# Within-chunk mLSTM products and token sums by 64 columns, gate products of all chunks in one, and 1/rms along tokens by DMA

## The chip, the cores and the metric

The kernel runs on one core of one Trainium2 chip. The metric is the device time of one execution, in microseconds (us). TensorE (PE) multiplies, VectorE (DVE) and ScalarE (ACT) do elementwise work, GpSimd (POOL) does small powers and memsets and issues part of the DMAs, SyncE (SP) issues the weight loads. A matmul keeps one operand in the array (stationary, loaded by a weight load, PEld) and streams the other through it. An f32 matmul appears in the trace as two passes, each with its own weight load; a transpose, and a matmul on the rounded fp32r type, is one pass.

## The reference

Two layers on x of 512 tokens by 1024. Each layer adds a mixer with four branches to x and then a squared-relu MLP; both read an RMSNorm of x. The parts that the change touches:

```python
def rms_norm(x, g):
    return x * lax.rsqrt(mean(x * x, -1) + EPS) * g

# mLSTM, chunks of 128 tokens, 4 heads of 64; i = c_i + i_bias, f = c_f + f_bias
b = cumsum(log_sigmoid(f))                       # within the chunk
dmat = where(tril, b_j - b_s + i_s, -inf)
mj = max(b + m_st, max_s dmat)
a = exp(dmat - mj) * (q @ k.T)
num = w_inter * (q @ c_st) + a @ v               # a @ v: the within-chunk product
den = w_inter * (q @ n_st) + sum(a)
h = num / max(abs(den), exp(-mj))
```

## The kernel before

The activations live feature-major, as 8 tiles of 128 features by 512 tokens. Every projection is a product of fp32 operands that are split in a high and a low fp32r part and multiplied in three passes (`mm3`: high·high, high·low, low·high). The weights stream from DRAM in chunks of mostly 512 KB: SP loads `raw` (two buffers), ACT casts it to `whi`, DVE subtracts to get `wlo` (three buffers each, `split_w`, lines 254 to 261). A layer is a fixed sequence of such products on PE: token-major groups (`tk`, 512, 336 or 256 columns), feature-major groups (`fm`), the gates (`g`, `p`), the output projection (`wo`), and the MLP (`up`, `q`, `r`).

All smaller work (indexer, attention, mLSTM, spatial gating, norms) is written as generators in a list `side`. After every half of a feature-major group, and twice per token-major weight chunk, `tick()` (lines 281 to 286) advances each generator to its next `yield`. What a generator issues is tied by `Paced` to the last projection pass before that tick, so it can't stand earlier than that on its engine. Within that, the order of each engine's queue is laid out when the program is built, by priority (`HP`, `Ahead`) and by when operands are due. At run time each queue is in order: an instruction that waits holds all behind it on its engine.

The places that the change touches:

- **Token sums.** `rstd2` (line 316) and `rstd` (line 332) get the mean square of each token: the sum of squares `acc` (128 by 512, over features) is multiplied by a column of 1/1024. The four blocks of 128 tokens of `acc` are the stationary operand, the moving one is a single column, and the result is `pa`, 128 tokens by 4. This is done four times: before each mixer and each MLP.
- **1/rms along tokens.** `rstd` raises the sums to the power -1/2 on POOL (`rs`, tokens on partitions), which the token-major projections use as a scale. For the feature-major ones it also needs 1/rms along the free axis on all partitions (`rb`, 128 by 512): lines 348 to 352 broadcast each column of `rs` as a stationary operand against the identity (`pb`, four f32 products) and ACT copies it to `rb`. The first reader is the `cqT` product of line 1171.
- **Gates.** `forget_gates` (line 905) computes the biased input gates `ip` and log-sigmoid forget gates `lf` for 128 tokens by 4 chunks by 4 heads, on DVE. `mlstm` (line 929) then takes the cumulative sum over a chunk twice: once with tokens on partitions (line 945, `bc`, one f32 product with the triangle `tri` as stationary), and once with heads on partitions (lines 958 to 960: for each chunk a product `br` with `lf` of that chunk, 4 columns, as stationary, and a transpose `ir` of `ip`). For each chunk DVE copies `br`, subtracts, and scans for the running maximum `Gr` (lines 961 to 967). `Gr` and the chunk maxima go through DRAM to be broadcast to all partitions (`MB`, `X`).
- **The within-chunk product.** In each chunk, lines 1033 to 1035 multiply the 128 by 128 matrix `X` of a head (stationary) by that head's 65 columns of values and ones (`vaug`), into `intra`. It follows the state product `inter` (64 rows of the array, from the second chunk on) and is followed, in the first three chunks, by the state update `U` (lines 1043 to 1045), whose 64 stationary columns go to one half of the output partitions or the other by head, as `half(h)` (line 662) says. The spatial gating's `mix` products (line 1233) are also of 64 columns.

POOL's queue holds, around the gates: the power `rs`, the tables `tab`, the power `va` of the indexer, the moves `qiA` and `qiB`, the power `ssq` of the query norm (line 1108), and the moves `qS`.

Of the kernel before, what the change touches and what calls it, by code (L numbers as in the profile page):

```python
# [13 lines left out]
F32 = mybir.dt.float32  # L14
# [7 lines left out]
P = 128  # L22
# [144 lines left out]
def trunk(tc, x_in, wall, consts, lps, sgus, out):  # L167
# [5 lines left out]
    with ExitStack() as es:  # L173
# [24 lines left out]
        xm_dram = [nc.dram_tensor(f"xm_{l}_dram", (KD, P, T), F32, kind="Internal").ap() for l in range(NL)]  # L198
        sum_dram = [nc.dram_tensor(f"sum_{l}_dram", (NC, P, D), F32, kind="Internal").ap() for l in range(NL)]
        gr_dram = [nc.dram_tensor(f"gr_{l}_dram", (4, T + 8), F32, kind="Internal").ap() for l in range(NL)]  # L200
        xs = [None]
# [69 lines left out]
        def pmm(o, a, b, start=True, stop=True):  # L271
            T_.matmul(o, a, b, start=start, stop=stop)
# [25 lines left out]
        def norm(x, gain, hh, hl, ks=range(KD), acc=None, sq_hp=True, sq_tile=None):  # L298
# [15 lines left out]
            return acc  # L314

        def rstd2(acc):

            r2 = small["t4"]

            def gen():  # L320
                yield
                yield
                pa = mmtile("pa", "ms")
                for c in range(NC):
                    pmm(pa[:, c:c + 1], acc[:, c * P:(c + 1) * P], ones)
# [6 lines left out]
        def rstd(acc, late=2):  # L332

            rs, t4 = small["rs"], small["t4"]
            rb = hpool.tile([P, T], F32, name="rb", tag="rb")

            def gen():
                for _ in range(late):
                    yield
                pa = mmtile("pa", "ms")  # L340
                for c in range(NC):
                    pmm(pa[:, c:c + 1], acc[:, c * P:(c + 1) * P], ones)
                with HP():
                    V.tensor_scalar(t4, pa[:, 0:4], EPS, None, ALU.add)
                    rpow(rs, t4)
                for _ in range(1 if late < 3 else 3):
                    yield
                pb = mmtile("pb", "ms")
                for c in range(NC):
                    pmm(pb[:, c * P:(c + 1) * P], rs[:, c:c + 1].to_broadcast([P, P]), ident)  # L350
                with HP():
                    S.copy(rb, pb)

            side.append(gen())
            return rs, rb
# [258 lines left out]
        for l in range(NL):  # L614
            with ExitStack() as em:
                x = mixer(tc, em, locals())
            hh, hl = htiles()
            r2 = rstd2(norm(x, lp("ln_mlp"), hh, hl))
            xs[0].close()
            if l < NL - 1:  # L620
                lpt = cpool.tile([P, NLP], F32, name="lp", tag="lp")
                nc.scalar.dma_start(lpt, lps[l + 1])
            nxt, acc = mlp(l, hh, hl, r2, lp("ln_mix"))
            if nxt:
                hh, hl = nxt
                rs, rb = rstd(acc, 8)
        flush()


def mixer(tc, em, env):  # L630
# [103 lines left out]
    else:  # L734
# [14 lines left out]
        load_consts()  # L749
        rs, rb = rstd(acc[0])  # L750
    qr = {}
# [153 lines left out]
    def forget_gates():  # L905
        s16 = [P, 4, 4]
        ip, lf, gc = (tt(s16, "c_" + n) for n in ("ip", "lf", "gc"))
        e5 = et("c_e")
# [16 lines left out]
        V.scalar_tensor_tensor(lf, pl, -2.0, fp, ALU.mult, ALU.add)  # L925
        lfs.extend((ip, lf, gc))
        yield

    def mlstm(yc):
# [11 lines left out]

        ip, lf, gc = lfs
# [12 lines left out]
        yield  # L955
        pr = mmtile("br", "ms")
        pi_ = mmtile("ir", "ms")
        for c in range(4):
            pmm(pr[0:4, blk(c)], lf[:, c], tri)
            ptr(pi_[0:4, blk(c)], ip[:, c])  # L960
        for c in range(4):
            br, gr = tt([4, P], "br"), tt([4, P], "gr")
            V.tensor_copy(br, pr[0:4, blk(c)])
            V.tensor_sub(gr, pi_[0:4, blk(c)], br)
            V.tensor_tensor_scan(Gr[:, blk(c)], gr, gr, ms8[:, c:c + 1], ALU.max, ALU.max)
            if c < 3:
                V.tensor_add(ms8[:, c + 1:c + 2], br[:, P - 1:P], Gr[:, c * P + P - 1:c * P + P])
        V.tensor_copy(ms8[:, 4:8], Gr[:, P - 1::P])

        G.dma_start(scr[:, 0:T], Gr)  # L970
        G.dma_start(scr[:, T:T + 8], ms8)
# [17 lines left out]
        for c in range(4):  # L989
            ptr(pe_[:, c * 4:c * 4 + 4], Gr[:, blk(c)])  # L990
        gcol = pe_[:, 0:16].rearrange("p (c h) -> p c h", h=4)
# [13 lines left out]
        for c in range(4):  # L1005
# [401 lines left out]
```

## Time and profile before

| | |
|---|---|
| median of 3 runs | 1596.76 us (1596.72 to 1596.97) |
| the profiled execution's own time | 1596.6 us |
| its span in the trace | 1594.8 us |
| PE busy | 1586.3 us, 99% of the span, 7510 passes |
| PEld, DVE, ACT, POOL busy | 82%, 70%, 45%, 8% |
| granted TensorE clock | 1.0 mean, 9 or more tenths in each of 40 slices |
| HBM traffic | 120 GB/s over the span |

The table's shares are means over the span. Passes on PE are pipelined: the time that a group of passes costs is read from start to start, not from the length of one pass. An idle time counts only where it is PE's.

### The profile page before, as it was taken

The numbers are of one execution on the slowest core, as the hardware profiler recorded it, in microseconds if no ns is written. First come the engines' busy times: TensorE is split into PE (matmuls) and PEld (weight loads), VectorE is DVE, ScalarE is ACT, GpSimd is POOL, SyncE is SP. The second block draws the span as 40 slices with busy tenths as digits, with TensorE's granted clock in tenths as the row PEclk, the third lists the DMA queues.
The fourth block names the chain that finished last, engine by engine and source line by source line (L and its number), as shares of the span: only waits on it lengthen the run. The fifth ranks groups of instructions, "written<-read, shape, count | busy, mean of one in ns | idle before, by whom it ended". The sixth has DMA issues, their size and how long they took to land.

```text
span 1594.8 us, 20013 instructions
## 1 busy us (share of the span) xinstructions
PE 1586.3 (99%) x7510; PEld 1310.9 (82%) x7510; DVE 1112.0 (70%) x1900; ACT 710.3 (45%) x1059; POOL 121.6 (8%) x141
## 2 busy tenths in 40 slices
PE   9999999999999999999999999999999999999998
PEld 8888888888888888888788888887888888888887
DVE  6899997545555655665988999975555557556568
ACT  5553234423345545635545432254233455456362
POOL 1212100000000100110013121000000001001100
PEclk9999999999999999999999999999999999999999
DMA  6433322242353473386443332322323524733844
GB/s 213 118 88 111 100 90 83 83 144 92 104 200 110 78 226 105 66 190 193 119 141 113 93 112 91 98 84 86 132 96 113 202 95 78 227 104 66 221 149 106
DMA packets 66129, 196.23 MB, mean 123 GB/s; under 512 B 7368, under 2 KB 14568, under 8 KB 66032
## 3 DMA queue, kind: packets, MB, share of 16 engines
q1 hardware_dynamic: 54160, 167.15, 31.7%
q0 software_dynamic: 11008, 26.79, 9.9%
q8 instruction: 59, 0.97, 0.2%
q10 hardware_dynamic: 864, 1.01, 0.2%
q14 instruction: 38, 0.31, 0.1%
HBM read 174.46 MB, written 16.79 MB: 120 GB/s over the span
## 4 chain that ended last, share of the span: by engine, by line
PE 88%; issue 9%; DMA 1%; POOL 1%; DVE 0%; ACT 0%; POOLq 0%; ACTq 0%; DVEq 0%
PE g L139 22%; PE up L139 16%; PE tk L139 11%; PE fm L139 8%; PE q L139 8%; PE p L139 6%; PE r L139 5%; PE wo L139 5%; DMA cr<-in_wall_dram 1%; PE ix L139 1%; POOL sum_dram L453 1%; PE lg L139 1%; PE av L139 1%; PE pT L139 1%; PE intra L139 0%
## 5 line engine op out<-in xcount | busy, mean ns | idle before, releaser
L139 DVE TENSOR_TENSOR wlo<-raw,whi 128x1024 fp32r<-128x1024 f32 (+3 forms) x221 | 283.6, 1284 | 136.0 <-ACT whi L139 135.9
L139 ACT CAST whi<-raw 128x1024 fp32r<-128x1024 f32 (+3 forms) x221 | 241.5, 1094 | 241.7 <-PE up L139 59.5
L139 PE MATMUL g<-hh,whi 128*128 128x512 f32 x512 | 200.7, 392 | 0.0
L139 PE MATMUL g<-hh,wlo 128*128 128x512 f32 x512 | 199.5, 390 | 0.0
L139 PE MATMUL up<-hh,whi 128*128 128x512 f32 x512 | 199.4, 389 | 0.0
L139 PE MATMUL g<-hl,whi 128*128 128x512 f32 x512 | 199.3, 389 | 0.0
L139 PE MATMUL up<-hh,wlo 128*128 128x512 f32 x512 | 199.2, 389 | 0.0
L139 PE MATMUL up<-hl,whi 128*128 128x512 f32 x512 | 199.2, 389 | 0.0
L139 DVE TENSOR_TENSOR wlo<-cr,whi 128x1024 fp32r<-128x1024 f32 x96 | 117.0, 1222 | 83.5 <-ACT whi L139 83.3
L139 ACT CAST whi<-cr 128x1024 fp32r<-128x1024 f32 x96 | 100.7, 1053 | 131.2 <-PE r L139 43.1
L139 ACT ACTIVATE gs<-gs 128x512 f32<-128x512 f32 x64 | 40.6, 635 | 198.6 <-DVE gs L139 195.4
L139 PEld LDWEIGHTS g<-hh,wlo 128*128 128x128 f32 x512 | 96.1, 188 | 20.3
L139 PEld LDWEIGHTS g<-hh,whi 128*128 128x128 f32 x512 | 96.1, 188 | 20.1 <-issue 0.3
L139 PEld LDWEIGHTS up<-hh,whi 128*128 128x128 f32 x512 | 96.1, 188 | 20.0
L139 PEld LDWEIGHTS up<-hh,wlo 128*128 128x128 f32 x512 | 96.1, 188 | 20.0
L139 PEld LDWEIGHTS up<-hl,whi 128*128 128x128 f32 x512 | 96.1, 188 | 19.8
L139 PEld LDWEIGHTS g<-hl,whi 128*128 128x128 f32 x512 | 96.2, 188 | 19.3
L139 PE MATMUL tk<-whi,hh 128*128 128x512 f32 (+2 forms) x304 | 108.3, 359 | 0.0
L139 PE MATMUL tk<-wlo,hh 128*128 128x512 f32 (+2 forms) x304 | 107.3, 353 | 0.0
L139 PE MATMUL tk<-whi,hl 128*128 128x512 f32 (+2 forms) x304 | 106.5, 352 | 0.0
L430 POOL DMA_DIRECT2D cr<-in_wall_dram x32 | 27.8, 867 | 955.9 <-DVE wlo L139 950.8
L139 DVE TENSOR_TENSOR gs<-g,rb 128x512 f32<-128x512 f32 x64 | 44.1, 688 | 80.8 <-PE g L139 80.6
(283 smaller groups left out, 3184.3 us busy)
## 6 DMA issues: line engine op xcount, KB each, us to landing
raw<-in_wall_dram SPq DMA_DIRECT2D x147, 512.0 KB, 3.5
raw<-in_wall_dram SPq DMA_DIRECT2D x64, 640.0 KB, 3.9
cr<-in_wall_dram SPq DMA_DIRECT2D x32, 512.0 KB, 5.3
cr<-in_wall_dram POOLq DMA_DIRECT2D x32, 512.0 KB, 5.4
x<-in_x_dram SPq DMA_DIRECT2D x16, 256.0 KB, 4.5
xm_dram<-x SPq DMA_DIRECT2D x16, 256.0 KB, 2.0
sum_dram<-co SPq DMA_DIRECT2D x16, 256.0 KB, 5.3
sum_dram<-co POOLq DMA_DIRECT2D x16, 256.0 KB, 7.4
```

The source lines that it names most:

```text
L139: r = f(*a, **k)
L430: nc.gpsimd.dma_start(dst, piece(i, j, k), accum_op=ALU.add)
L453: nc.gpsimd.dma_start(dst, tiles[b], accum_op=ALU.add)
```

## The change

1. The four token sums are computed in halves of 64 tokens: eight products with 64 stationary columns, alternately into partitions 0 to 63 and 64 to 127, in place of four with 128 (`token_sums`).
2. `rb` is no longer made by PE and ACT: POOL's queue issues a DMA of `rs` to DRAM (element by element transposed) and a second that reads it back, broadcast to 128 partitions.
3. The cumulative sums of the gates move from `mlstm` into `forget_gates`, two ticks after the gates. `ip` and `lf` are stored head-major as 128 by 16, so that one product gives all chunks with heads and chunks on partitions (16 rows) and one transpose gives `ip`. DVE copies and subtracts once on 16 partitions. Two DMAs on POOL's queue bring the 16 rows through DRAM to 4 partitions (`gi`). `mlstm` loses one `yield` and starts at the scans.
4. The within-chunk product is made in two halves of 64 stationary columns for each head.

```diff
+        rs_dram = [nc.dram_tensor(f"rs_{l}_dram", (NC, P), F32, kind="Internal").ap() for l in range(NL)]
+        gi_dram = [nc.dram_tensor(f"gi_{l}_dram", (4, 4, P + 1), F32, kind="Internal").ap() for l in range(NL)]
...
+        def token_sums(pa, acc):
+
+            for c in range(NC):
+                for i in range(2):
+                    t = c * P + i * 64
+                    pmm(pa[i * 64:i * 64 + 64, c:c + 1], acc[:, t:t + 64], ones)
...
-                for c in range(NC):
-                    pmm(pa[:, c:c + 1], acc[:, c * P:(c + 1) * P], ones)
+                token_sums(pa, acc)
...
                 with HP():
                     V.tensor_scalar(t4, pa[:, 0:4], EPS, None, ALU.add)
                     rpow(rs, t4)
-                for _ in range(1 if late < 3 else 3):
-                    yield
-                pb = mmtile("pb", "ms")
-                for c in range(NC):
-                    pmm(pb[:, c * P:(c + 1) * P], rs[:, c:c + 1].to_broadcast([P, P]), ident)
-                with HP():
-                    S.copy(rb, pb)
+                G.dma_start(rs_dram[l].rearrange("c p -> p c"), rs)
+                G.dma_start(rb, rs_dram[l].rearrange("c p -> (c p)").partition_broadcast(P))
...
     def forget_gates():
         s16 = [P, 4, 4]
-        ip, lf, gc = (tt(s16, "c_" + n) for n in ("ip", "lf", "gc"))
+
+        cols = [tt([P, 16], "c_" + n) for n in ("ip", "lf")]
+        ip, lf = (t.rearrange("p (h c) -> p c h", c=4) for t in cols)
+        gc = tt(s16, "c_gc")
...
-        lfs.extend((ip, lf, gc))
+        yield
+        yield
+
+
+        pb = mmtile("bc", "ms")
+        pmm(pb[:, 0:16], tri, cols[1])
+        pmm(pb[0:16, 128:256], cols[1], tri)
+        ptr(pb[0:16, 256:384], cols[0])
+        V.tensor_sub(gc, ip, pb[:, 0:16].rearrange("p (h c) -> p c h", c=4))
+        t16 = tt([16, P + 1], "t16")
+        V.tensor_copy(t16[:, 0:P], pb[0:16, 128:256])
+        V.tensor_sub(t16[:, 0:P], pb[0:16, 256:384], t16[:, 0:P])
+        V.tensor_copy(t16[:, P:], pb[0:16, 255:256])
+        gi = tt([4, 4, P + 1], "gi")
+        rows = env["gi_dram"][l]
+        G.dma_start(rows.rearrange("h c t -> (h c) t"), t16)
+        G.dma_start(gi, rows)
+        lfs.extend((ip, gc, gi))
         yield
...
-        pb = mmtile("bc", "ms")
-        pmm(pb[:, 0:16], tri, lf.rearrange("p c h -> p (c h)"))
-        V.tensor_sub(gc, ip, pb[:, 0:16].rearrange("p (c h) -> p c h", h=4))
+        ip, gc, gi = lfs
...
-        Gr = tt([4, T], "Gr")
+        Gr = gi[:, :, 0:P]
...
-        yield
-        pr = mmtile("br", "ms")
-        pi_ = mmtile("ir", "ms")
         for c in range(4):
-            pmm(pr[0:4, blk(c)], lf[:, c], tri)
-            ptr(pi_[0:4, blk(c)], ip[:, c])
-        for c in range(4):
-            br, gr = tt([4, P], "br"), tt([4, P], "gr")
-            V.tensor_copy(br, pr[0:4, blk(c)])
-            V.tensor_sub(gr, pi_[0:4, blk(c)], br)
-            V.tensor_tensor_scan(Gr[:, blk(c)], gr, gr, ms8[:, c:c + 1], ALU.max, ALU.max)
+            V.tensor_tensor_scan(Gr[:, c], Gr[:, c], Gr[:, c], ms8[:, c:c + 1], ALU.max, ALU.max)
             if c < 3:
-                V.tensor_add(ms8[:, c + 1:c + 2], br[:, P - 1:P], Gr[:, c * P + P - 1:c * P + P])
+                V.tensor_add(ms8[:, c + 1:c + 2], gi[:, c, P:], Gr[:, c, P - 1:])
...
             pn = mmtile("intra", "ms")
             for h in range(4):
-                pmm(pn[:, h * 65:(h + 1) * 65], X[:, h], vaug[:, c, h])
+                for i in range(2):
+                    pmm(pn[half(i), h * 65:(h + 1) * 65], X[:, h, i * 64:i * 64 + 64], vaug[:, c, h])
```

## Rows read from the trace of the kernel before

**Rows 1.** The profile page: busy time and share of PE, and the granted clock.

```profile
PE 1586.3 (99%) x7510; PEld 1310.9 (82%) x7510; DVE 1112.0 (70%) x1900; ACT 710.3 (45%) x1059; POOL 121.6 (8%) x141
PEclk9999999999999999999999999999999999999999
```

**Rows 2.** PE's waits by releaser: us in total, times, longest us.

```profile
PE warm L139 <- ACT warm L139: 2.7, 1, 2.7
PE r L139 <- DVE wlo L139: 1.2, 2, 0.8
```

**Rows 3.** Timeline of PE, first chunk: start us, us, engine, line, operation, out<-in.

```profile
160.35 1.00 PE L139 MATMUL intra<-vaug,X 128*128 128x65 f32 x8
...
161.28 0.45 PE L139 MATMUL U<-vaug,kw 128*64 128x65 f32 x8
...
161.57 1.04 PE L139 MATMUL mix<-wt,v 128*64 128x128 f32 x16
...
162.54 0.50 PE L139 MATMUL fm<-hh,whi 128*128 128x512 f32 x1
```

**Rows 4.** Timeline of PE, second chunk, behind the state product.

```profile
183.48 1.11 PE L139 MATMUL intra<-vaug,X 128*128 128x65 f32 x8
184.51 0.45 PE L139 MATMUL U<-vaug,kw 128*64 128x65 f32 x8
184.90 0.50 PE L139 MATMUL g<-hh,whi 128*128 128x512 f32 x1
```

**Rows 5.** Timeline of PE: a group of 64 columns entered from a projection.

```profile
153.44 0.39 PE L139 MATMUL fm<-hh,wlo 128*128 128x512 f32 x1
153.76 1.09 PE L139 MATMUL mix<-wt,v 128*64 128x128 f32 x16
```

**Rows 6.** Timeline of PE: the broadcast of 1/rms, in both layers.

```profile
36.91 1.13 PE L139 MATMUL pb<-cst,rs 128*128 128x128 f32 x8
...
37.79 0.40 PE L139 MATMUL tk<-whi,hh 128*128 128x336 f32 x1
...
829.55 1.06 PE L139 MATMUL pb<-cst,rs 128*128 128x128 f32 x8
830.36 0.40 PE L139 MATMUL tk<-wlo,hh 128*128 128x336 f32 x1
```

**Rows 7.** Timeline of PE: two of the four pairs of gate products.

```profile
122.55 0.38 PE L139 MATMUL br<-cst,c_lf 128*4 128x128 f32 x2
...
123.06 0.38 PE L139 MATMUL br<-cst,c_lf 128*4 128x128 f32 x2
```

**Rows 8.** Timeline of PE: the token sums before the first and the second mixer.

```profile
27.68 0.95 PE L139 MATMUL pa<-ones,acc 128*128 128x1 f32 x8
...
28.49 0.40 PE L139 MATMUL tk<-whi,hh 128*128 128x336 f32 x1
...
816.33 0.50 PE L139 MATMUL pa<-ones,acc 128*128 128x1 f32 x4
825.18 0.61 PE L139 MATMUL pa<-ones,acc 128*128 128x1 f32 x4
```

**Rows 9.** Timeline: third tick of the indexer's transposes, and the last forget-gate instruction.

```profile
47.95 0.60 PE L139 MATMUL qiT<-cst,qr 128*128 128x128 f32 x4
...
51.92 0.16 DVE L139 SCALAR_TENSOR_TENSOR c_lf<-c_e 128x16 f32<-128x16 f32 x1
```

**Rows 10.** Timeline: the power on POOL, the weight split behind it, its reader on PE.

```profile
57.51 2.93 POOL L139 TENSOR_TENSOR ssq<-ssq,nhalf 128x16 f32<-128x16 f32 x1 [2.35 <-DVE ssq L139]
...
61.97 1.22 DVE L139 TENSOR_TENSOR wlo<-raw,whi 128x1024 fp32r<-128x1024 f32 x1
...
68.42 0.40 PE L139 MATMUL fm<-hh,whi 128*128 128x512 f32 x1
```

**Rows 11.** DMA issues (KB each, median us to landing), and the first reader of rb.

```profile
MB<-gr_dram POOLq DMA_DIRECT2D x2, 16.0 KB, 4.1
...
68.15 0.69 DVE L139 TENSOR_TENSOR cqT<-fm,rb 128x512 f32<-128x512 f32 x1 [0.22 <-PE fm L139]
```

More of the change, by code (lines that the diff above doesn't have):

```diff
@@ L330, in rstd2, with rstd @@
             return r2
-        def rstd(acc, late=2):
+        def rstd(acc, l, late=2):
             rs, t4 = small["rs"], small["t4"]
@@ L340, in gen @@
                 pa = mmtile("pa", "ms")
-                for c in range(NC):
-                    pmm(pa[:, c:c + 1], acc[:, c * P:(c + 1) * P], ones)
+                token_sums(pa, acc)
                 with HP():
@@ L345, in gen @@
                     rpow(rs, t4)
-                for _ in range(1 if late < 3 else 3):
-                    yield
-                pb = mmtile("pb", "ms")
-                for c in range(NC):
-                    pmm(pb[:, c * P:(c + 1) * P], rs[:, c:c + 1].to_broadcast([P, P]), ident)
-                with HP():
-                    S.copy(rb, pb)
+                G.dma_start(rs_dram[l].rearrange("c p -> p c"), rs)
+                G.dma_start(rb, rs_dram[l].rearrange("c p -> (c p)").partition_broadcast(P))
             side.append(gen())
@@ L625, in trunk @@
                 hh, hl = nxt
-                rs, rb = rstd(acc, 8)
+                rs, rb = rstd(acc, l + 1, 8)
         flush()
@@ L749, in mixer @@
         load_consts()
-        rs, rb = rstd(acc[0])
+        rs, rb = rstd(acc[0], 0)
     qr = {}
@@ L940, in finish @@
                 V.scalar_tensor_tensor(yl, pk[:, blk(j)], mn[:, j:j + 1], yh.bitcast(F32), ALU.mult, ALU.subtract)
-        ip, lf, gc = lfs
-        pb = mmtile("bc", "ms")
-        pmm(pb[:, 0:16], tri, lf.rearrange("p c h -> p (c h)"))
-        V.tensor_sub(gc, ip, pb[:, 0:16].rearrange("p (c h) -> p c h", h=4))
+        ip, gc, gi = lfs
         ms8 = tt([4, 8], "ms8")
         V.memset(ms8, 0.0)
-        Gr = tt([4, T], "Gr")
+        Gr = gi[:, :, 0:P]
         E3 = tt([P, 4, 14], "E3")
@@ L954, in mlstm @@
         scr = env["gr_dram"][l]
-        yield
-        pr = mmtile("br", "ms")
-        pi_ = mmtile("ir", "ms")
         for c in range(4):
-            pmm(pr[0:4, blk(c)], lf[:, c], tri)
-            ptr(pi_[0:4, blk(c)], ip[:, c])
-        for c in range(4):
-            br, gr = tt([4, P], "br"), tt([4, P], "gr")
-            V.tensor_copy(br, pr[0:4, blk(c)])
-            V.tensor_sub(gr, pi_[0:4, blk(c)], br)
-            V.tensor_tensor_scan(Gr[:, blk(c)], gr, gr, ms8[:, c:c + 1], ALU.max, ALU.max)
+            V.tensor_tensor_scan(Gr[:, c], Gr[:, c], Gr[:, c], ms8[:, c:c + 1], ALU.max, ALU.max)
             if c < 3:
-                V.tensor_add(ms8[:, c + 1:c + 2], br[:, P - 1:P], Gr[:, c * P + P - 1:c * P + P])
-        V.tensor_copy(ms8[:, 4:8], Gr[:, P - 1::P])
-        G.dma_start(scr[:, 0:T], Gr)
+                V.tensor_add(ms8[:, c + 1:c + 2], gi[:, c, P:], Gr[:, c, P - 1:])
+        V.tensor_copy(ms8[:, 4:8], Gr[:, :, P - 1])
+        G.dma_start(scr[:, 0:T].rearrange("h (c t) -> h c t", c=4), Gr)
         G.dma_start(scr[:, T:T + 8], ms8)
@@ L989, in mlstm @@
         for c in range(4):
-            ptr(pe_[:, c * 4:c * 4 + 4], Gr[:, blk(c)])
+            ptr(pe_[:, c * 4:c * 4 + 4], Gr[:, c])
         gcol = pe_[:, 0:16].rearrange("p (c h) -> p c h", h=4)
```

## The prediction, made before the changed kernel ran

> **What bounds the kernel now.** I read the busy table first, then what PE waited for, then the timeline of PE around each group that the change touches. PE is busy 99% of the span at the full granted clock in every slice, while DVE is at 70% and POOL at 8% [rows 1]. PE's waits come to a few us in all: the largest is 2.7 us at the start, the next 1.2 us in the MLP [rows 2]. So nothing feeds PE too slowly, and a us taken out of PE's in-order stream is a us off the end, as long as no operand becomes late. The 7510 passes [rows 1] over the span of 1594.8 us give 0.21 us from start to start on average; I use that as the ordinary step between passes. The changed parts are all on this stream, so each is priced from start to start: a group costs the time from its first pass to the first projection pass behind it. DVE's and ACT's savings are costed at nothing, because PE covers them.
>
> **Within-chunk products.** Before, a head is two passes with 128 stationary columns. In the first chunk the eight passes take 161.28 - 160.35 = 0.93 us [rows 3]. After, there are sixteen passes with 64 columns, alternately in the two halves of the array's columns. That form is in the trace: U has 64 columns, the same 65 moving ones, and heads that alternate between the halves, and its eight passes take 161.57 - 161.28 = 0.29 us, 0.036 us each [rows 3]. Sixteen make 0.58 us. Going from full to half columns isn't free: the mix group starts 0.32 us behind the projection pass ahead of it [rows 5], 0.11 us over the ordinary step. Leaving costs too: from U to the next projection pass are 0.39 us [rows 4], 0.10 us over its 0.29. So per layer:
> - First chunk: 0.93 - 0.58 - 0.11 = 0.24 us gained, since the change of mode ahead of U only moves forward.
> - Second and third chunk: before, the intra group takes 184.51 - 183.48 = 1.03 us [rows 4], with the change to half columns in it; after, it follows the state product, which needs a change in either version. 1.03 - 0.58 = 0.45 us each.
> - Fourth chunk, with no U behind: 0.93 - 0.58 - 0.10 = 0.25 us.
>
> That is 1.39 us a layer, 2.8 us in two. The bounds: if N sets the pitch more than I think, the nearest row is mix, (162.54 - 161.57)/16 = 0.061 us a pass with 128 moving columns [rows 3], and sixteen take 0.97 us, so the gain is about 0 (a loss of 0.2 us a layer). Above, I see no reason for more than U's pitch. I take U's: it has the same shape.
>
> The trace shows about 0.1 us for a change of mode. The Trainium skill, TensorEngine Tiling (Array Packing), Key Properties, states that changing the tiling mode drains TensorE. Read as a wait for a whole pass in flight it would speak against splitting small groups; that reading is the first rival.
>
> **1/rms along tokens.** The eight passes of pb disappear, with their copy on ACT: 37.79 - 36.91 = 0.88 us in the first layer, 830.36 - 829.55 = 0.81 us in the second [rows 6]. Sum 1.7 us. In their place come two DMAs on POOL's queue. The nearest row for small scattered pieces is MB, 4.1 us to landing [rows 11]; two in a row make 8.2 us. `rs` exists a few us after the sums that begin at 27.68 [rows 8], so `rb` lands around 40 us, and its first reader runs at 68.15 [rows 11]. The latency is covered by over 25 us; without that cover each layer would lose up to 8.2 us.
>
> **Gates.** The pairs of gate products repeat every 123.06 - 122.55 = 0.51 us [rows 7]. One pair of four remains (16 stationary columns in place of 4), so three go: 1.53 us a layer, 3.1 us in two. The product with the triangle as stationary is there in both versions and only moves: 0. Each layer's two DMAs and four small DVE operations have the whole stretch from the gates' end at 52.08 us [rows 9] to the scans, which come behind the pairs of 122.55 [rows 7]; were that cover gone, 8.2 us of latency would stand in each layer; the four copies and four subtractions on 4 partitions that DVE loses are worth nothing, as DVE isn't the bound.
>
> **Token sums.** Before, 28.49 - 27.68 = 0.81 us [rows 8]. After, sixteen passes at 0.036 = 0.58 us, plus 0.11 and 0.10 for the change in and out: 0.79 us, nothing gained. In the second layer the sum stands in two pieces (at 816.33 and 825.18 [rows 8]) and pays the change twice: 0.2 us lost. No row shows 64 columns against a single moving column. Bounds: a quarter of the full-width pitch (0.81/8/4 = 0.025 us) gives 0.40 + 0.21 = 0.61 us, 0.8 us gained in four sums; the pitch of mix gives 0.97 + 0.21 = 1.18 us, 1.5 us lost. I take -0.1 us, between the ends and from U, the nearest shape.
>
> **The sum.** 2.8 + 1.7 + 3.1 - 0.1 = 7.5 us. The profiled execution took 1596.6 us, 0.16 us under the median of 1596.76. 1596.6 - 7.5 = 1589.1; on the median's footing 1589.3, and I give **1589.2 us**, 0.47% faster.
>
> **What the new waits hold up.** POOL waits in order, so the read-back of each pair of DMAs holds POOL until the first has landed, 4.1 us [rows 11]. Behind the rs pair stand the tables and the indexer's power, behind the gates' pair the query norm's power ssq. DVE in turn waits for ssq (it ends at 60.44), and the weight split at 61.97 stands behind that wait on DVE; PE reads that split from 68.42 [rows 10]. It ends at 63.19, so the cover is 5.2 us, and one landing of 4.1 us fits in it.
>
> **Rivals.**
> - *The halves give nothing.* Each change to half columns costs as much as a full pass in flight, and the intra gain of 2.8 us and up to 1.5 us in the token sums go. Then 7.5 - 2.8 - 1.4 = 3.3 us remain: 1593.3 us, still just faster. Against it: U, at 0.036 us a pass, with mode changes of 0.1 us around it. 7%.
> - *PE waits for the forget gates.* Their group now comes two ticks after the gates' first tick, which is the tick of the indexer's third transposes, at 47.95. The last gate instruction ends at 52.08 on DVE [rows 9]. Placed there, PE would stand 4.1 us in each layer, 8.2 us in all, and the gain is gone: 1597.4 us, no change by the bound below. Against it: the second layer's token sum stands in two pieces 9 us apart [rows 8], so a group's place on PE follows its operands, not the program text. 8%.
> - *POOL's queue becomes the bound (slower).* The transposed store of rs is 512 pieces of 4 bytes, and the gates' pair is just ahead of ssq. If a landing takes three times MB's, 12.3 us, and ssq is behind it, DVE's weight split is 12.3 - 5.2 = 7.1 us late for PE, 14.2 us in two layers: 1589.2 + 14.2 = 1603.4 us. It decides against the change (slower by 0.2%) from a landing of about 10.6 us. For it: POOL's and DVE's order is strict. Against it: MB, in 32-byte pieces, lands in 4.1 us, and 10.6 is far from that. 4%. The Trainium skill, DMA: Bandwidth & Descriptors, Rules for kernel authors, has a strided last dimension lowered to one descriptor per element, which speaks for this rival; no run here shows such a DMA yet.
> - *Another engine takes over.* With PE ahead by some us, weights come late in the stretch where DVE is nearly full, and half of the gain is lost: 1593 us. Against it: PE's only waits for a weight split come to 1.2 us [rows 2]. 4%.
>
> **How the numbers follow.** My forecast has 77%. A measurement of this kernel can tell about 0.2%, 3.2 us, from no change. Faster by more than that: the forecast, and most of the first and last rival, 0.85. Within: the gates rival and what falls short of the line, 0.10. Slower: POOL's queue, 0.05. The range is 1587.0 to 1593.5: below, the bound of the token sums (0.9 us) and another us because the projection passes right behind a removed group also start late today; above, the halves giving nothing (1593.3). Left out are the second and third rival and some rest.
>
> **What would show it.** Right: pb gone, one group of bc, br and ir per layer; intra as x16 of 128*64 with about 0.036 us from start to start; token sums at about 0.8 us; PE's waits unchanged. Wrong: an intra group of 0.9 us or more (the halves run one after the other); a new wait of PE for the gates' tile near 48 to 53 us; a wait of PE for wlo near 68 us with POOL's ssq moved back; a DVE wait for rb.

## The result, and the profile after

The changed kernel takes 1608.86 us in the median (1608.22 to 1610.18, four runs) against 1596.74 us of the kernel before: a ratio of 1.0075, 95% interval 1.0063 to 1.0087. It is slower by 12 us where 7.5 us less were forecast. The profiled execution has a span of 1606.4 us.

The page's busy table of the changed kernel, then its waits of PE (us in total, times, longest):

```profile
PE 1583.7 (99%) x7572; PEld 1305.8 (81%) x7572; DVE 1110.2 (69%) x1890; ACT 708.8 (44%) x1057; POOL 119.2 (7%) x149
```

```profile
PE bc L139 <- DVE c_lf L139: 11.9, 2, 6.4
PE warm L139 <- ACT warm L139: 2.7, 1, 2.7
PE pT L139 <- DVE L L139: 1.7, 2, 0.9
PE r L139 <- DVE wlo L139: 1.4, 2, 0.8
...
```

PE's busy time fell by 2.6 us [rows 1], although there are 62 more passes, and still the end came later: two waits that were not there before [rows 2] take 11.9 us. The timeline of PE in the first layer shows where the new gates' group stands and what comes behind it:

```profile
50.25 0.39 PE L139 MATMUL tk<-whi,hl 128*128 128x512 f32 x1
57.01 0.58 PE L139 MATMUL bc<-c_lf,cst 128*128 128x16 f32 x2 [6.37 <-DVE c_lf L139]
57.52 0.61 PE L139 MATMUL bc<-cst,c_lf 128*16 128x128 f32 x2
...
58.66 0.63 PE L139 MATMUL tk<-wlo,hh 128*128 128x512 f32 x1
59.09 0.63 PE L139 MATMUL tk<-whi,hl 128*128 128x512 f32 x1
```

The group is queued twelve projection passes, some 3 us, behind the third transposes (at 47.27 us here), near the place that the second rival named, and PE stands 6.37 us there. The projection passes behind it follow at 0.43 us in place of 0.23: the clock has fallen. The windows say the same (columns: us, busy time of PE, PEld, DVE, ACT, POOL, granted clock, DMA share, GB/s):

```profile
30.00:36.00 6.00, 6.00 (x42) 6.00 (x41) 2.15 (x4) 2.39 (x4) 1.63 (x2) 1.00 1.03 100
36.00:42.00 6.00, 6.00 (x35) 5.32 (x35) 1.16 (x2) 2.41 (x7) 0.35 (x1) 1.00 0.63 31
...
54.00:60.00 6.00, 2.99 (x10) 2.19 (x11) 4.89 (x13) 1.17 (x2) 2.81 (x6) 0.54 0.76 205
60.00:66.00 6.00, 6.00 (x27) 4.91 (x26) 3.46 (x9) 0.74 (x2) 3.30 (x5) 0.89 0.33 90
```

The first two windows tell what came earlier: between 30 and 36 us the DMA engines are full (share 1.03) and move only 100 GB/s; in the kernel before they were at 0.52 and moved 176 GB/s there:

```profile
30.00:36.00 6.00, 6.00 (x41) 6.00 (x40) 2.67 (x4) 2.72 (x4) 1.55 (x3) 1.00 0.52 176
```

This is the time of the transposed store of `rs`. POOL's timeline, and the DMA issues between 28 and 48 us (KB each, median us to landing), of the changed kernel:

```profile
29.48 1.15 POOL L139 TENSOR_TENSOR rs<-t,nhalf 128x4 f32<-128x4 f32 x1
30.94 1.00 POOL L139 DMA_DIRECT2D rs_dram<-rs  x1 [0.31 <-POOL rs L139]
41.65 0.59 POOL L139 DMA_DIRECT2D rb<-rs_dram  x1 [9.71 <-DMA rs_dram<-rs]
42.26 1.25 POOL L139 TENSOR_TENSOR tab<-cst,lp 128x256 f32<-128x256 f32 x2
```

```profile
raw<-in_wall_dram SPq DMA_DIRECT2D x4, 512.0 KB, 6.1
rb<-rs_dram POOLq DMA_DIRECT2D x1, 256.0 KB, 5.9
rs_dram<-rs POOLq DMA_DIRECT2D x1, 2.0 KB, 10.1
```

The store of 2 KB takes 10.1 us, and the weight loads in flight beside it 6.1 us; in the kernel before they take 3.5 us in the same stretch. The Trainium skill, DMA: Bandwidth & Descriptors, Anatomy of one DMA, fits a DMA as 2.0 us plus bytes over bandwidth; for 2 KB that gives an estimate of 2.0 us, and the measured 10.1 us decides against it for pieces of 4 bytes. ACT and DVE then show who was held up. First the changed kernel, then the one before:

```profile
44.32 1.05 ACT L139 CAST whi<-raw 128x1024 fp32r<-128x1024 f32 x1 [5.31 <-DMA raw<-in_wall_dram]
45.40 1.22 DVE L139 TENSOR_TENSOR wlo<-raw,whi 128x1024 fp32r<-128x1024 f32 x1 [6.53 <-ACT whi L139]
56.69 0.17 DVE L139 SCALAR_TENSOR_TENSOR c_lf<-c_e 128x16 f32<-128x16 f32 x1
```

```profile
39.58 1.04 ACT L139 CAST whi<-raw 128x1024 fp32r<-128x1024 f32 x1
40.66 1.23 DVE L139 TENSOR_TENSOR wlo<-raw,whi 128x1024 fp32r<-128x1024 f32 x1 [1.11 <-ACT whi L139]
```

The cast waits for its load and comes 4.74 us later, the split behind it on DVE as well, and the gate chain, which stands behind that split in DVE's queue, ends at 56.69 us in place of 51.92 [rows 9]: 4.77 us late. So the page gives a chain: store, weight load, cast, split, gates, PE. It does not yet exclude another: POOL stands 9.71 us at the read-back, and the indexer's tables behind it come late too.

The groups on PE that were to become cheaper did. PE's timeline of the changed kernel, token sums of the first layer, then the first chunk:

```profile
28.29 0.63 PE L139 MATMUL pa<-ones,acc 128*64 128x1 f32 x16
28.85 0.42 PE L139 MATMUL tk<-whi,hh 128*128 128x336 f32 x1
```

```profile
164.00 0.69 PE L139 MATMUL intra<-vaug,X 128*64 128x65 f32 x16
164.52 0.40 PE L139 MATMUL U<-vaug,kw 128*64 128x65 f32 x8
164.85 0.50 PE L139 MATMUL fm<-hh,whi 128*128 128x512 f32 x1
```

The token sums take 28.85 - 28.29 = 0.56 us against 0.81 [rows 8]. The sixteen intra passes take 0.52 us, 0.032 us each, against 0.93 for eight before [rows 3]; but fm follows U at once, where before the mix group did.

### The profile page after: what moved, and what is told of

The parts are those of the page before. It is cut to its first block, busy times and chain, and to the rows that moved or that the text cites. A ratio compares the mean times of both kernels' runs of the same rounds, so it can differ in the third digit from the quotient of the medians.

```text
span 1606.4 us, 20127 instructions
## 1 busy us (share of the span) xinstructions
PE 1583.7 (99%) x7572; PEld 1305.8 (81%) x7572; DVE 1110.2 (69%) x1890; ACT 708.8 (44%) x1057; POOL 119.2 (7%) x149
## 3 DMA queue, kind: packets, MB, share of 16 engines
q0 software_dynamic: 11360, 27.36, 10.1%
## 4 chain that ended last, share of the span: by engine, by line
PE 84%; DVE 6%; issue 5%; DMA 2%; POOL 1%; ACT 1%; DVEq 0%; POOLq 0%; ACTq 0%
PE up L139 19%; PE g L139 18%; PE tk L139 9%; PE q L139 9%; PE fm L139 8%; PE r L139 6%; PE wo L139 5%; PE p L139 5%; DVE wlo L139 2%; PE ix L139 1%; DMA cr<-in_wall_dram 1%; DMA raw<-in_wall_dram 1%; DVE sco L139 1%; PE lg L139 1%; PE pT L139 1%
## 5 line engine op out<-in xcount | busy, mean ns | idle before, releaser
L139 PE MATMUL q<-whi,ah 128*128 128x512 f32 x256 | 99.7, 393 | 0.0
L139 PE MATMUL q<-wlo,ah 128*128 128x512 f32 x256 | 99.7, 389 | 0.0
```

Of the source, the lines that this page charges most:

```text
L139: r = f(*a, **k)
```

## The experiments

Ratios are to the kernel before, run on the same chip. "Net cost" of a group is the time from the start of the projection pass ahead of it to the start of the second one behind it, less the two ordinary steps in that stretch.

**Where the loss comes from.** Five kernels each undo or alter one part.

```diff
# gates_later: the changed kernel, gates' group four ticks later
-        yield
-        yield
+        yield from wait(6)
         pb = mmtile("bc", "ms")
```

> The changed kernel with six yields in place of two ahead of the gates' group of products. Theory (PE comes to the group before the forget gates are there; the store of rs in 4-byte pieces makes the weight load, and with it DVE's gate chain, late; the clock falls in the wait): PE no longer waits for c_lf (11.9 us gone in two layers), the granted clock is 1.0 in every stretch, about 4.6 us of passes at the lower clock go as well, 1590 to 1593 us. Rival (the store and the held POOL queue slow the stretch wherever the group stands): PE waits for weights or other operands in place of c_lf, over 1600 us.

Measured: 1595.49 us, ratio 0.9988 (0.9978 to 0.9997), 2.5 us over the range that the theory gave. No wait for the gates; the group's net cost is 0.68 us where bc, br and ir took 2.26 before. The store still holds up the cast (it waits 6.05 us for its load), and some of that turns into small new waits:

```profile
PE pT L139 <- DVE L L139: 2.4, 2, 1.3
PE fm L139 <- ACT vt L139: 1.2, 2, 0.8
```

So the place of the group decides whether the late gates cost PE anything.

```diff
# rb_on_pe: the changed kernel with pb back; its place for the gates is kept
-                G.dma_start(rs_dram[l].rearrange("c p -> p c"), rs)
-                G.dma_start(rb, rs_dram[l].rearrange("c p -> (c p)").partition_broadcast(P))
+                for _ in range(1 if late < 3 else 3):
+                    yield
+                pb = mmtile("pb", "ms")
+                for c in range(NC):
+                    pmm(pb[:, c * P:(c + 1) * P], rs[:, c:c + 1].to_broadcast([P, P]), ident)
+                with HP():
+                    S.copy(rb, pb)
```

> The changed kernel with rb made by PE and ACT as in the kernel before, without the two DMAs; the gates' group stays two ticks behind the gates. Theory: the weight load after the token sums lands in 3 to 4 us again, the gate chain on DVE ends 4 to 5 us earlier, PE's wait for c_lf falls from 6.4 and 5.6 us to 1.5 to 2 us each, too short for the clock to fall; pb costs 2.0 us: 1596 to 1599 us. Rival (the group's place alone makes the wait): the wait stays at 5 to 6 us, and with pb the time is about 1611 us.

Measured: 1595.16 us, ratio 0.9989 (0.9979 to 0.9998), clock at full speed. The gates' wait falls to 0.8 us in each layer. The early place alone therefore costs 1.7 us of waits in two layers; the other 10.2 us come with the DMAs.

```diff
# readback_late: the changed kernel, read-back six ticks behind the store
                 G.dma_start(rs_dram[l].rearrange("c p -> p c"), rs)
+                for _ in range(6):
+                    yield
                 G.dma_start(rb, rs_dram[l].rearrange("c p -> (c p)").partition_broadcast(P))
```

> The changed kernel with the read-back of rb issued six ticks behind the store, so that POOL isn't held while the store is under way; the store itself is unchanged. Theory (the store's small pieces hold the DMA engines and delay the weight load): the wait for c_lf stays within 1 us of 6.4 and 5.6, the time within 2 us of 1608.9. Rival (POOL, held for the landing, makes tables and powers late, and so DVE): the wait falls to 2 us or less, 1595 to 1599 us.

Measured: 1609.76 us, ratio 1.0081 (1.0066 to 1.0096), waits of 5.7 and 6.8 us. It settles nothing: in POOL's queue the read-back still stood ahead of the tables, so POOL was held 8.78 us all the same.

```diff
# rows_store: rs turned on PE, stored as 4 rows of 512 bytes
+                for _ in range(1 if late < 3 else 3):
+                    yield
+                pb = mmtile("pb", "ms")
+                ptr(pb[0:4, 0:P], rs)
+                r4 = small["r4"][0:4]
+                with HP():
+                    V.tensor_copy(r4, pb[0:4, 0:P])
-                G.dma_start(rs_dram[l].rearrange("c p -> p c"), rs)
+                G.dma_start(rs_dram[l], r4)
```

> The changed kernel with rs transposed on PE first (one pass for each layer) and copied, so that the store is 4 rows of 512 bytes in place of 512 pieces of 4 bytes; POOL still waits for it. Theory: the store lands in 3 to 4 us in place of 10, the weight load isn't delayed, the wait for c_lf is 1.5 to 2.5 us each and the clock doesn't fall: 1595 to 1598 us. Rival (POOL held): the hold is still 4 us of the 10, so the wait is 3 to 4 us each and the clock falls: 1600 to 1604 us.

Measured: 1597.35 us, ratio 1.0003 (0.9994 to 1.0012), gates' waits 1.9 and 2.1 us in the profiled execution. Its DMA issues between 20 and 60 us:

```profile
raw<-in_wall_dram SPq DMA_DIRECT2D x7, 512.0 KB, 3.5
...
rs_dram<-r POOLq DMA_DIRECT2D x1, 2.0 KB, 2.5
```

The same 2 KB in rows of 512 bytes land in 2.5 us and leave the weight loads at 3.5; the cast that came at 44.32 us in the changed kernel starts at 39.64, as before. So a trip through DRAM need not cost anything here. But the store also comes later, at 38.72 us in place of 30.94, since it waits for the transpose and its copy. Loads ran beside it there too (132 GB/s between 38 and 42 us), yet this run alone changes the form of the store and its hour together.

```diff
# dead_store: rb_on_pe, with the store still issued and read by nobody
+                G.dma_start(rs_dram[l].rearrange("c p -> p c"), rs)
```

> The changed kernel with 1/rms along tokens back on PE (as in the second experiment, which had a ratio of 0.9989 and waits for the forget gates of 0.8 us), but with the store of rs in 4-byte pieces still issued; nothing reads it, so POOL never waits for it. Theory (the store slows the weight loads in flight, ACT's cast and with it DVE's gate chain come late): the waits for the forget gates come back, 4 to 6 us in each layer, with the clock falling behind them, the first cast behind its load some 4 us later than before, and a time of 1604 to 1610 (ratio 1.004 to 1.008). Rival (POOL held at the read-back makes DVE late): waits of 0.8 us as without the store, 1595 to 1596 (ratio about 0.999).

Measured: 1610.05 us, ratio 1.0079 (1.0066 to 1.0093). This is the experiment that settles the cause. POOL isn't held; its timeline, the cast on ACT, and the wait of PE:

```profile
31.54 1.00 POOL L139 DMA_DIRECT2D rs_dram<-rs  x1 [0.31 <-POOL rs L139]
32.55 2.25 POOL L139 TENSOR_TENSOR tab<-cst,lp 128x256 f32<-128x256 f32 x2
```

```profile
45.77 1.05 ACT L139 CAST whi<-raw 128x1024 fp32r<-128x1024 f32 x1 [5.11 <-DMA raw<-in_wall_dram]
```

```profile
PE bc L139 <- DVE c_lf L139: 11.7, 2, 6.1
```

The tables follow the store at once, and the cast, the gates and PE are as late as in the changed kernel. The whole loss comes back with 512 elements of 4 bytes that nothing waits for: what costs is the delay of the weight loads beside the store, not its latency and not POOL's order. The DMA queues between 28 and 48 us (packets, MB, share of the 16 engines' time), of the kernel before and of this one; q1 carries SP's loads, q0 the store:

```profile
q1 hardware_dynamic: 616, 2.20, 32.8%
```

```profile
q1 hardware_dynamic: 576, 2.07, 68.1%
q0 software_dynamic: 32, 0.00, 0.3%
```

The loads move a little less and hold the engines for twice the time, while the store's own packets, listed as 32, hold them for 0.3%. So the engines don't show as busy with the elements; the loads' packets last longer beside them. The Trainium skill, DMA: Bandwidth & Descriptors, Queues, rings and completion order, says that each DMA engine takes turns between its queues packet by packet; that fits loads of 9.4 in place of 3.5 us beside the store, but no run here shows what lengthens the packets.

**What the lower clock costs.** The changed kernel with the wait filled with work: 27 products of 512 columns on PE, written to the gates' own tile and overwritten. (The third `yield` leaves the group in its place, twelve projection passes behind the third transposes.)

```diff
-        yield
-        yield
+        yield from wait(3)
         pb = mmtile("bc", "ms")
+        for _ in range(27):
+            T_.matmul(pb, hh[0][:, 0:P], hh[0], start=True, stop=True)
```

> The changed kernel with 27 idle products of 512 columns (their results are overwritten) on PE in the place where it waits for the forget gates; they take 6.1 us, about the wait. Theory (a part of the loss is the lower clock behind a wait of 6 us): the clock stays at 1.0, the wait nearly disappears, and the about ten passes behind it take 0.23 in place of 0.43 us: 2.0 to 2.6 us a layer, 1603 to 1605.5 us. Rival (the passes behind the wait are slow for another reason, such as late weights): they stay slow and the time is 1608 to 1610 us.

Measured: 1604.58 us, ratio 1.0045 (1.0032 to 1.0059), clock 0.999. PE's wait for the gates falls from 11.9 to 0.8 us in all, filled with work that is worth nothing, and the time falls too: 0.0030 of 1597 us is 4.8 us (the two intervals just part). The traces agree: from the first product of the gates to the transposes `kiT` behind the group, the changed kernel takes 5.41 and 6.03 us in the two layers, this one 3.50 and 3.54, 4.4 us less. So the clock that falls behind the two waits costs some 4 to 5 us on top of the 11.9.

**1/rms by DMA alone, on the kernel before** (the `G.dma_start` pair, store and read-back, in place of pb).

> The kernel before with rb made by the store of rs and the broadcast read-back, and nothing else; the gates stay in the mLSTM part, 60 us later. Theory (the store makes the weights and DVE late, but without a group that PE needs at once most of it is hidden): the weight load behind the store lands late by 4 to 5 us, PE's own waits are 1 to 3 us in all, pb's 2.0 us are saved: within 1.5 us of the kernel before. Rival (the store costs PE by itself): PE waits for weights of 5 us or more and the kernel is 4 us or more slower than before.

Measured: 1601.04 us, ratio 1.0024 (1.0014 to 1.0033), 3.8 us slower, between the two expectations. Without the gates' group in its way the late DVE reaches PE elsewhere, by ACT, and the clock falls there as well (third from the end of each row):

```profile
PE fm L139 <- ACT vt L139: 2.4, 2, 1.8
```

```profile
63.00:66.00 3.00, 2.18 (x7) 1.78 (x8) 0.72 (x4) 1.13 (x4) 2.65 (x1) 0.82 0.00 0
66.00:69.00 3.00, 3.00 (x10) 2.34 (x9) 2.68 (x8) 1.34 (x4) 0.28 (x1) 0.61 0.00 0
```

The clock isn't the whole of it: three of the ten executions have a mean clock of 1.0 and take 1600.8 to 1601.8 us all the same. This part of the change loses in either place.

**What the parts that gain are worth.** First both repairs together (pb on PE, gates' group two ticks later than in the change):

> The changed kernel with rb made by PE and ACT as in the kernel before, and four yields in place of two ahead of the gates' group. Theory: PE waits for c_lf no more (1.7 us in the second run of this study), no store delays the weights; against the kernel before the within-chunk product gives 2.5 to 2.9 us, the token sums 0.5, the gates 2.9 to 3.1: 4 to 6 us faster than before, ratio 0.9962 to 0.9975. Rival (PE is by now ahead of DVE in the mixer, so time saved on PE comes back as waits for DVE): PE's waits for L, vt and rel grow by what the group saves, and the ratio stays at 0.9985 or above.

Measured: 1594.07 us, ratio 0.9980 (0.9971 to 0.9989): 3.2 us faster than before, under the 4 to 6 us of the theory. The remaining parts should have given more; each alone, on the kernel before:

```diff
# intra_only
-                pmm(pn[:, h * 65:(h + 1) * 65], X[:, h], vaug[:, c, h])
+                for i in range(2):
+                    pmm(pn[half(i), h * 65:(h + 1) * 65], X[:, h, i * 64:i * 64 + 64], vaug[:, c, h])
```

> The kernel before with the within-chunk product in halves of 64 stationary columns, and nothing else. Theory (the halves run beside each other, 0.036 us a pass): 2.6 to 2.9 us faster, ratio 0.9982 to 0.9984. Rival (the halves give nothing, a change of mode costs a whole pass): within 0.5 us of the kernel before.

Measured: 1598.18 us, ratio 1.0007 (0.9998 to 1.0015), nothing. Yet the net costs of the four groups of a layer fall by 0.37, 0.57, 0.57 and 0.27 us, and at 242 us PE is 1.8 us ahead of where it would be. Then it waits, between 252 and 265 us and again in the second layer:

```profile
PE pT L139 <- DVE L L139: 1.5, 2, 0.9
PE lg L139 <- DVE yl L139: 1.2, 2, 0.6
```

> The kernel before with the gates of all chunks in one product, four ticks behind the gates in place of two, and nothing else of the change. Theory (three pairs of passes at 0.51 us go, and DVE loses work as well): the group costs 0.7 us in place of 2.26, so 3.1 us a run; part of it may come back as waits for L, so 1.5 to 3.1 us faster, 1594 to 1595.5 on the footing of 1597.3. Rival (all PE time saved ahead of the attention comes back as waits for DVE): same as before within 1 us, with PE waits for L and yl of about 3 us.

(The diff is the change's own for the gates, with four ticks in place of two.) Measured: 1595.47 us, ratio 0.9991 (0.9983 to 1.0000), 1.7 us of the 3.2. A part is lost by the `yield` that mlstm lost: the mix group of the first chunk stands by itself, and intra with U, and mix, have net costs of 1.42 and 1.23 us where together they had 2.30. Another part shows on the weight loads' row, not on PE's:

```profile
64.34 0.19 PEld L139 LDWEIGHTS fm<-hh,whi 128*128 128x128 f32 x1 [0.52 <-ACT vt L139]
64.71 0.19 PEld L139 LDWEIGHTS fm<-hh,whi 128*128 128x128 f32 x1 [0.18 <-ACT vt L139]
```

In that version POOL's power ssq [rows 10] stands behind the store of the gates' rows, and DVE gets it at 62.46 us in place of 60.48, 1.1 us late when both are counted from the start of their runs; DVE, ACT's `vt` and the weight loads follow, 0.7 us a layer.

```diff
# gates_behind_ssq: pb on PE, gates' group later still, mlstm's yield put back
-        yield
-        yield
+        yield from wait(12)
...
         scr = env["gr_dram"][l]
+        yield
```

> The changed kernel with 1/rms back on PE, the gates' group twelve ticks behind the gates (its two DMAs come behind the power ssq on POOL and behind the moves qS), and the yield that mlstm lost put back, so that in the first chunk the products of 64 columns stand together again. Theory (POOL's ssq behind the gates' DMAs cost 0.7 us a layer through DVE's rt, ACT's vt and PE's weight load; the separate mix group 0.3): that wait gone, up to 1.0 us a layer earlier until the attention, where part is given back to the fourth chunk's norm on DVE; 0.5 to 2 us under the version with four ticks, a ratio of 0.9967 to 0.9977. Rival (what is saved ahead of the attention all comes back as a wait for L): the same ratio, 0.998, with PE waits for L of 2 to 3 us in all.

Measured: 1595.75 us, ratio 0.9990 (0.9981 to 0.9999). The 0.7 us are gone and the 64-column groups stand together; by 234 us PE is 3.2 us ahead of the kernel before, counted from its start, more than in any version so far. By 265 us 2.7 of these are given back. PE's new waits in the two layers are 2.5 us for L, 1.2 for yl and 0.6 for gs; the rest stands on the weight loads. The rival was right that the saving doesn't arrive: more time saved ahead of the attention isn't more time saved.

**Who takes it back.** A control first: the scaling of the attention's rows moved from DVE to ACT, on the kernel before, and then with the halves.

```diff
-            V.tensor_scalar(L[:, :W], L[:, :W], se, None, ALU.mult)
+            S.activation(L[:, :W], L[:, :W], AF.Identity, scale=se)
```

> The kernel before with one change that has nothing to do with the one studied: the scaling of the attention rows by 1/sum (one DVE pass over up to 512 columns per head, chunk and branch) is done by ACT. It is the control for the next kernel. Theory (in the stretch of indexer and attention DVE is full, so PE time saved there comes back as waits for DVE's softmax): no wait of PE for DVE's L or yl in the kernel before, so DVE's relief alone gives nothing, within 1.5 us of before. Rival (DVE's lateness there has no bearing): also no change. The two part on the next kernel.

> The control with the halved within-chunk products, and nothing else of the change. Theory (DVE is full in the attention's stretch): with DVE relieved, the waits of PE for L and yl (1.5 and 1.2 us in the kernel with the halves alone) are gone, and the 1.8 us a layer that the intra groups save reach the end: 2.5 to 3.6 us under the control. Rival (the saved time is lost whatever DVE does, at the next product whose operand has a time of its own): within 1 us of the control, with waits of PE of some 2.5 us in another place.

Measured: 0.9999 (0.9990 to 1.0008) for the control and 0.9991 (0.9982 to 1.0000) with the halves, 1.4 us apart, between the two expectations: yl's waits are gone, those for L remain (1.7 us, now behind ACT). The same edit on the version with both repairs (whose gates' group stands two ticks later than in the changed kernel, four behind the gates):

> The changed kernel with 1/rms back on PE, the gates' group four ticks later, and the attention's scaling on ACT. Theory (what was left of DVE's bound in that version, 0.9 us of waits for L and what DVE's work delays behind it, goes): 1 to 2 us under that version, 1592 to 1593.5 on the footing of 1597.3, ratio about 0.9970. Rival (ACT, which casts the weights, becomes late in turn): the same or slower than that version, ratio 0.998 or more, with PE waits for whi or wlo.

Measured: 0.9982 (0.9973 to 0.9991), no better than without it. This edit shortens the work behind the stretch, not in it. So the next three take work out of the stretch: they leave out two of sixteen top-k rounds, which changes the result, and so tell about time alone.

```diff
         for r in range(16):
-            V.max(m8, sco)
-            V.match_replace(sco, m8, sco, SENT)
+            if r < 14:
+                V.max(m8, sco)
+                V.match_replace(sco, m8, sco, SENT)
```

> The kernel before with 14 of the 16 top-k rounds of each chunk (the last two are left out), which takes about 7 us a layer off DVE's full stretch and nothing off PE. It is the control for the next two. Both theories: PE has no wait for DVE in the attention of the kernel before, so no change within 1 us.

> The control (14 top-k rounds) with the halved within-chunk products, and nothing else of the change. Theory (DVE's full queue is what takes the saving back): no wait of PE for L and yl, and the whole 3.6 us of the two layers reach the end: 3 to 4 us under the control. Rival (it is taken back by what follows, whatever DVE has to do): within 1 us of the control, with waits for L and yl of 2 to 3 us in all.

> The control (14 top-k rounds) with the whole change except 1/rms by DMA, the gates' group behind ssq and the yield put back. Theory: with DVE relieved, the 3.1 us a layer that PE had saved by 240 us reach the end nearly whole: 5.5 to 6.5 us under the control, ratio about 0.996 to it. Rival: about 1.5 us under the control, as without the relief, with waits of 3 us or more for L, yl and gs.

Measured: the control 1597.02 us, 1.0001 (0.9992 to 1.0010): DVE's relief alone is worth nothing. With the halves 1593.99 us, 0.9979 (0.9970 to 0.9988): 3.0 us under the control, where without the relief they gave nothing. With everything but the DMA of `rs` 1590.28 us, 0.9956 (0.9944 to 0.9969): 6.7 us under the control. The waits for L, yl and gs are gone; all that is left of PE's waits with the halves:

```profile
PE warm L139 <- ACT warm L139: 2.7, 1, 2.7
PE r L139 <- DVE wlo L139: 1.5, 2, 0.8
PE xT L139 <- DVE co L139: 0.8, 1, 0.8
```

Windows from 200 to 240 us, of the kernel before and of the halves with the short top-k (DVE is the third busy time): 39.72 of 40 us against 36.89; the control has 37.86.

```profile
200.00:240.00 40.00, 40.00 (x206) 32.74 (x205) 39.72 (x87) 13.24 (x18) 1.01 (x1) 1.00 0.27 84
```

```profile
200.00:240.00 40.00, 40.00 (x226) 32.59 (x225) 36.89 (x80) 13.33 (x18) 1.31 (x2) 1.00 0.25 85
```

DVE's queue ahead of the attention is what took the savings back.

**A version that keeps them.** Nothing left out: gates_behind_ssq, with some 3.7 us a layer of DVE's work moved to ACT.

```diff
-        V.tensor_scalar(sq, sq, 0.044715, 1.0, ALU.mult, ALU.add)
+        S.activation(sq, sq, AF.Identity, scale=0.044715, bias=1.0)
...
-        V.tensor_scalar(v2[c // 2][:, s_], v2[c // 2][:, s_], vs[:, c:c + 1], 0.5, ALU.mult, ALU.mult)
+        S.activation(v2[c // 2][:, s_], v2[c // 2][:, s_], AF.Identity, scale=vs[:, c:c + 1])
...
-        V.tensor_scalar(t, z, cw[:, 4 + i:5 + i], None, ALU.mult)
+        S.activation(t, z, AF.Identity, scale=cw[:, 4 + i:5 + i])
```

(`vs` is halved once ahead of that, and the attention's scaling is on ACT as above.)

> The version with 1/rms on PE, the gates' group behind ssq and the yield put back, and some 3.7 us a layer of DVE's work between 120 and 250 us moved to ACT with nothing left out: the scale and offset in the gelu (four of 0.41 us), the scaling of the gating's values (1.2 us for four, less one small operation), the first tap of the convolution (two of 0.5) and the attention's scaling. Theory (DVE's queue takes the savings back, as with the short top-k): half or more of the 2.7 us a layer that were given back remain; 2 to 5 us under the version without the relief, 1591 to 1594 on the footing of 1597.2, ratio 0.996 to 0.998, waits for L, yl and gs under 2 us in all. Rival (ACT, whose order is strict as well, becomes late with casts or reads in turn): no faster than 0.998, with waits for whi, or for DVE behind ACT.

Measured: 1592.41 us, ratio 0.9972 (0.9961 to 0.9983): 4.8 us faster than before, the lowest median of all kernels here that compute everything (its interval overlaps that of 0.9980 above), and 16 us under the changed one. Its waits of PE:

```profile
PE warm L139 <- ACT warm L139: 2.7, 1, 2.7
PE g L139 <- DVE gs L139: 1.5, 2, 0.8
PE r L139 <- DVE wlo L139: 1.2, 2, 0.6
...
```

L and yl no longer hold PE; gs, one step earlier, does a little.

## Why the prediction was wrong, step by step

- **Within-chunk products: right in mechanism, a little small, and not at the end.** U's pitch of 0.036 us was the right row; measured 0.032. The net costs fell by 0.57, 0.57 and 0.27 us in the second to fourth chunk where 0.45, 0.45 and 0.25 stood. The first chunk, with 0.24 us, gave nothing in the changed kernel: the yield that mlstm lost put the mix group behind projection passes, with changes of mode of its own; kept together it gave 0.37. The first rival (nothing from halves) is excluded.
- **1/rms along tokens: the step that failed.** The sum had "pb gone, 1.7 us", and PE did save 2.0 us (net cost 1.06 and 0.90). The price of the two DMAs was put at a latency, by MB's 4.1 us, with 25 us of cover. Wrong in size: 10.1 us for the store alone. Wrong in kind, which matters more: the latency was covered, and what cost was the weight loads beside the store, 6.1 us to landing in place of 3.5, and with them the cast, the gates and 11.9 us of PE's waits. [rows 11] shows a landing and no occupancy; the store, a form with no row, should have had a bound through the loads that run beside it.
- **Gates: the gain right, the place wrong.** 3.1 us were forecast, and the net cost fell by 1.58 us a layer, 3.2 in two, where no wait stands in it (gates_later). The rival "PE waits for the forget gates" had the mechanism and nearly the place, and got 8%, on the ground that a group's place follows its operands. It follows the operands' planned times, fixed at build: the group stands twelve projection passes behind the third transposes in the changed kernel and in rb_on_pe alike, though the gates end some 4 us earlier in the second. Its price of 4.1 us a layer counts from the transposes and so leaves out those twelve passes: with the loads in time the place costs 0.8 us (rb_on_pe), and with them late 6.4 and 5.6.
- **Token sums.** -0.1 us forecast, a gain of 0.5 us measured in four sums (net cost 0.91 to 0.76 for a whole one, 1.17 to 1.07 for the one in two pieces): U's pace holds with one column too (0.56 us for sixteen passes with the way out), and the sum after came out as forecast, 0.76 for 0.79. Mispriced was the sum before: 0.81 us leaves out its way in and out, which the 0.79 contains.
- **"A us off PE's stream is a us off the end."** It holds with no operand late, and the prediction said so, but checked it only by PE's waits of before [rows 2]. A wait of zero says nothing of the slack behind it. Between 200 and 240 us DVE had 0.28 of 40 us left in the kernel before, and the attention's operands stand behind that work; the 70% of [rows 1] hid it. The rival "another engine takes over" was this one, with 4%, and describes the change without its DMA: 3.2 us of gain were left with both repairs, 1.6 with the group behind ssq.
- **POOL's queue (the rival on the slower side).** It named the right DMA and the right sign, and got the wrong way in: the dead store shows the loss with POOL free. Its threshold of 10.6 us for a landing has therefore no meaning; the landing was 10.1.

The sum as it came: gains of about 2.8 (intra) + 2.0 (pb) + 3.2 (gates) + 0.5 (sums) = 8.5 us; against these 11.9 us of waits for the gates, 4.8 for the clock behind them and 1.9 for other new waits (pT 1.7, r 0.2), 18.6 together. The difference, 10.1 us, stands against 11.6 between the spans; of the 1.5 us left, 0.5 lie in the first 10 us of the program (PE waits 0.4 us for its first cast; this start, at the lower clock, differs by up to 1.2 us between the kernels), and 1.0 is not placed.

## What to carry to other kernels

A small DMA is not free because its landing is covered: count its pieces, look at what else the DMA engines carry at that hour, and write rows rather than elements, even if a transpose on PE makes them. (Here leaving the products on PE was no worse than the rows: 0.9989 against 1.0003.) In a queue whose order is fixed at build, a group moved ahead needs its operand's time with a margin, since a wait there costs its own length and, as here behind 5.6 to 6.8 us, the clock behind it. Before a saving on a full engine is counted, look for the next meeting with an engine that is nearly as full, and measure that one's slack in the stretch, not over the span.

## What the runs showed of the hardware that was not expected

- A store of 512 elements of 4 bytes landed in 9.2 to 11.0 us in six kernels. The median landing of the 512 KB loads between 28 and 48 us went from 3.5 to 6.1 us in the changed kernel, and to 9.4 with the dead store, where the loads held the DMA engines for 68.1% of that stretch in place of 32.8% and the store's own packets for 0.3%; 4 pieces of 512 bytes landed in 2.5 us.
- PE's clock fell to its lower level (1.2 GHz; passes at 0.43 us) behind waits of 5.6 to 6.8 us in three kernels, and in one kernel behind 1.8 us of wait (mean 0.61 between 66 and 69 us), but not behind 1.9 and 2.1 us in another, rows_store (1.00 in the stretch). That is one profiled execution of each: of the ten executions of rows_store four have a mean clock of 0.997 to 0.998, against 0.999 and more in the others, which suggests that behind such short waits it falls in one execution of a kernel and not in the next; the traces of those four are not kept. No run tells what decides.
